# A pool of short columns (128 bytes a partition) is opened in front of the pool of split weights

## The chip, the core and the metric

The kernel runs on one core of a Trainium2 chip. The metric is the device time of one execution, in microseconds (us). Each engine of the core has its own instruction stream: TensorE (PE in the profile, with its weight loads as PEld), VectorE (DVE), ScalarE (ACT), GpSimd (POOL) and SyncE (SP, which issues most of the DMAs).

## The reference

One sequence of 256 tokens of width 1024 goes through five stages, all in float32:

```python
x = x + hgrn_gmlp_mixer(x)     # mixer 0: x@w_in (1024 x 3072), gated recurrence, gMLP, @w_out
x = x + peer_ffn(x)            # 16384 experts, 8 heads, top 16 of each
x = x + mla_moba_mixer(x)      # mixer 1: two kinds of attention, @w_out
x = x + peer_ffn(x)
# second block: z = rmsnorm(x) @ w_in (1024 x 8192); pooling branch, dilated attention, gates
x = x + (gate_a * (y_a @ w_proj_a) + gate_b * (y_b @ w_proj_b)) @ w_out
return rmsnorm(x) * final_gain
```

In `peer_ffn` each token takes, for each of 8 heads, the 16 best of 16384 experts; the output is the sum over the chosen experts of gate * gelu(x . down[e]) * up[e].

## The kernel before

**Products of split numbers.** A float32 product is made of three float32r matmuls (`mm3`, lines 423 to 426): every operand is kept as a high part and a low part, and hi\*hi, hi\*lo and lo\*hi are added up in PSUM. The parts of the weights are made on the core by `split_weights` (line 484): ScalarE writes the high part `wh` from the loaded block, VectorE (sometimes GpSimd) writes the low part `wl`. One block is 128 partitions by 1024 floats, 4096 bytes in each partition.

**Where these parts lie.** The pool `ws` (line 376) has five buffers of `wh` and five of `wl`, opened once in `Net.__init__` and used by all five stages. The mixers have a small pool `w` of their own beside it (three more pairs), and `Stream.advance` gives each unit of weights a buffer of the one or the other. Loaded, unsplit blocks lie in `raw` (expert tables) and `wraw` (the other weights). `esm` (line 379) holds the short columns of the norms that join two stages: `ess` (16 bytes), `ev`, `ey` and `ea` (4 bytes each), each in a place of 32 bytes.

**The expert stage** (`peer`, line 1086, run twice) does not gather experts. It goes over all 128 blocks of 128 experts. `project(e)` makes 24 matmuls of 256 columns per block, with `xh` or `xl` (the token vectors) as the moving operand and `wh` or `wl` of the down table as the stationary one: tiles `ps<-xh,wh`, `ps<-xl,wh`, `ps<-xh,wl`. 40 blocks are projected while VectorE picks the top 16 (`front`), 60 while the gates are spread over the experts by one-hot matmuls (`acc<-oo,ah`), and 28 in the last part. That last part, `expand(e, tb, n)`, makes 12 matmuls of 512 columns per block, with `wh` or `wl` of the up table moving and the gated activations `W` (hi and lo of one block) stationary: tiles `acc<-wh,W` and `acc<-wl,W`. For the last four blocks all of these parts lie in one tile of another pool, called `places`, and the same 12 matmuls are shown as `acc<-places`.

**Mixers and the second block** run lists of `Lin` jobs. A job of kind "T" has the tokens moving and the weights stationary (`acc<-xh,wh`), one of kind "N" has the weights moving and the tokens stationary (`acc<-wh,xh`); 24 matmuls make one output piece. `N2` is the output product of a mixer, 512 columns wide (`acc<-wh,mh`).

All matmuls are recorded at line 421. The order is written out by hand (`manual_schedule`); each engine works through its own list in order.

Of the kernel before, what the change touches and what calls it, by code (L numbers as in the profile page):

```python
# [109 lines left out]
class Lin:  # L110
# [5 lines left out]
    def __init__(self, x, W, nk, cols, cn, kind, cb, late=0, k0=0, acc=None, start=True, stop=True,  # L116
                 need=None, mid=None, of=None, pieces=None):
        self.x, self.W, self.nk, self.cn, self.kind, self.cb, self.late = x, W, nk, cn, kind, cb, late
        self.mid, self.of = mid, of
        self.pieces = pieces or range({"T": cn // 128, "N": 2, "N2": 4}[kind])  # L120
        self.k0, self.acc, self.start, self.stop, self.need = k0, acc, start, stop, need
        self.cols = cols if isinstance(cols, tuple) else (cols, cn, 1, cn)
        self.w, self.keep = [], False
        if of:
            of.keep = True
# [240 lines left out]
class Net:  # L366
    def __init__(self, ctx, tc, A):
        self.tc, self.nc, self.A, self.ctx = tc, tc.nc, A, ctx
        nc = self.nc
        P = lambda name, **k: ctx.enter_context(tc.tile_pool(name=name, **k))  # L370
        self.cp = P("consts", bufs=1)
        self.raw = P("raw", bufs=4)
        self.dram = P("dram", bufs=1, space=DRAM)
        self.n = 0
        cp = self.cp
        self.ws = P("ws", bufs=WS)
        self.pa = P("pa", bufs=4, space=PSUM)
        self.pb = P("pb", bufs=4, space=PSUM)
        self.esm = P("esm", bufs=1)
        self.xn = [cp.tile([128, KB, S], F32R, name=n) for n in ("xh", "xl")]  # L380
        self.ident = cp.tile([128, 128], F32, name="ident")
        nc.scalar.dma_start(self.ident, A["c_ident"])
        self.vec = cp.tile([128, NVEC], F32, name="vec")
        self.entry = self.brow = None
# [1502 lines left out]
```

## Time and profile before

| what | value |
|---|---|
| time, median of 3 runs | 2179.43 us (2176.91 to 2179.50) |
| the profiled execution's own time | 2180.57 us |
| its span on the core | 2178.5 us |
| PE busy | 2122.6 us (97%) |
| DVE busy | 1568.8 us (72%) |
| ACT busy | 1125.7 us (52%) |
| mean granted clock of TensorE | 0.994 of full speed |

A matmul's duration in the profile is modelled and reaches beyond the start of the next one, so the rate of TensorE is read here from the starts: the time between two starts, called the pace below. Where a pace is worked out from rows of the timeline, it is the difference of two start times divided by the number of matmuls between them.

### The profile page before, as it was taken

The page shows a single profiled execution, that of the slowest core. Times are in us where ns is not written, and L with a number is a line of the kernel's source. Part 1 is how long each engine was busy: PE and PEld are TensorE (multiplying, and loading weights), DVE is VectorE, ACT ScalarE, POOL GpSimd, SP SyncE. Part 2 cuts the span into 40 slices and gives each one's busy share as a digit, 9 for nine tenths or more (in the row PEclk, how much of TensorE's full clock was granted, in tenths as well). Part 3 has the DMA queues.
Part 4 walks back from the last instruction along what each step waited for, and adds up shares of the span by engine and source line. Part 5 has one row for each costly group of instructions (what it writes and reads, how often), then busy time and mean ns, then how long its engine had stood idle before and what let it go on. Part 6 is the DMA issues. An engine that isn't in the chain of part 4 may idle for free.

```text
span 2178.5 us, 37618 instructions
## 1 busy us (share of the span) xinstructions
PE 2122.6 (97%) x14793; PEld 1932.1 (89%) x14793; DVE 1568.8 (72%) x2898; ACT 1125.7 (52%) x1944; POOL 215.7 (10%) x133
## 2 busy tenths in 40 slices
PE   7899999999999999998999999999999999999998
PEld 6879999999888888987799999998888889899998
DVE  7968978997555565668679789986666656644565
ACT  6245655554444444557455655555555555554443
POOL 2520110000000000013202200000000000122223
PEclk9999999999999999999999999999999999999999
DMA  7555454455666665744264545446666657475443
GB/s 233 185 185 184 145 194 146 156 159 161 188 189 190 188 195 192 260 129 148 87 233 135 195 149 162 155 155 188 189 187 190 194 193 261 148 218 153 136 146 115
DMA packets 165581, 382.19 MB, mean 175 GB/s; under 512 B 13137, under 2 KB 82444, under 8 KB 165148
## 3 DMA queue, kind: packets, MB, share of 16 engines
q1 hardware_dynamic: 160544, 364.95, 53.0%
q0 software_dynamic: 4672, 14.76, 1.9%
q8 instruction: 116, 1.90, 0.4%
q14 instruction: 61, 0.50, 0.1%
q10 hardware_dynamic: 188, 0.09, 0.0%
HBM read 376.56 MB, written 8.43 MB: 177 GB/s over the span
## 4 chain that ended last, share of the span: by engine, by line
PE 86%; DVE 9%; ACT 3%; issue 1%; DMA 0%; DVEq 0%; ACTq 0%
PE acc L421 53%; PE ps L421 29%; DVE wl L488 2%; ACT wh L487 1%; PE bsc L421 1%; PE bo L421 1%; DVE qL L678 1%; PE ps L200 1%; PE sc L421 0%; PE bpt L1747 0%; DVE eq L1278 0%; DVE s L1195 0%; DVE CI L1200 0%; DVE SC L658 0%; ACT scr L873 0%
## 5 line engine op out<-in xcount | busy, mean ns | idle before, releaser
L488 DVE TENSOR_TENSOR wl<-raw,wh 128x1024 fp32r<-128x1024 f32 x484 | 600.0, 1249 | 135.2 <-ACT wh L487 134.4
L421 PE MATMUL acc<-wh,W 128*128 128x512 f32 x1984 | 630.8, 395 | 0.0
L421 PE MATMUL ps<-xh,wh 128*128 128x256 f32 x2048 | 579.1, 283 | 0.0
L421 PE MATMUL ps<-xl,wh 128*128 128x256 f32 x2048 | 572.9, 280 | 0.0
L421 PE MATMUL ps<-xh,wl 128*128 128x256 f32 x2048 | 572.6, 280 | 0.0
L487 ACT ACTIVATE wh<-raw 128x1024 fp32r<-128x1024 f32 x504 | 526.9, 1054 | 74.2 <-PE ps L421 55.4
L421 PEld LDWEIGHTS acc<-wh,W 128*128 128x128 f32 x1984 | 373.4, 188 | 85.6 <-DVE W L1431 0.4
L421 PE MATMUL acc<-wl,W 128*128 128x512 f32 x992 | 391.5, 395 | 0.0
L421 PEld LDWEIGHTS ps<-xh,wh 128*128 128x128 f32 x2048 | 385.2, 188 | 2.4
L421 PEld LDWEIGHTS ps<-xl,wh 128*128 128x128 f32 x2048 | 385.1, 188 | 2.1
L421 PEld LDWEIGHTS ps<-xh,wl 128*128 128x128 f32 x2048 | 385.2, 188 | 0.0
L421 PEld LDWEIGHTS acc<-wl,W 128*128 128x128 f32 x992 | 186.7, 188 | 42.0 <-DVE wl L488 0.3
L1430 ACT ACTIVATE W<-ZB 128x256 fp32r<-128x256 f32 x168 | 91.4, 544 | 184.7 <-PE acc L421 161.0
L487 ACT ACTIVATE wh<-wraw 128x1024 fp32r<-128x1024 f32 (+1 forms) x140 | 144.4, 1043 | 46.5 <-PE acc L421 38.2
L1431 DVE TENSOR_TENSOR W<-ZB,W 128x256 fp32r<-128x256 f32 x168 | 89.8, 534 | 108.4 <-ACT W L1430 108.4
L488 DVE TENSOR_TENSOR wl<-wraw,wh 128x1024 fp32r<-128x1024 f32 (+2 forms) x104 | 132.8, 1284 | 45.9 <-ACT wh L487 45.7
L421 PE MATMUL acc<-xh,wh 128*128 128x256 f32 x480 | 136.2, 284 | 0.0
L421 PE MATMUL acc<-xh,wl 128*128 128x256 f32 x480 | 133.4, 278 | 0.0
L421 PE MATMUL acc<-xl,wh 128*128 128x256 f32 x480 | 133.3, 278 | 0.0
L181 POOL TENSOR_TENSOR ZB<-X,gain 128x512 f32<-128x512 f32 x4 | 5.2, 1293 | 1293.9 <-ACT ZB L179 1293.9
L1474 ACT ACTIVATE ZB<-acc 128x352 f32<-128x352 f32 (+30 forms) x128 | 47.7, 373 | 123.1 <-PE acc L421 119.3
L421 PE MATMUL acc<-wh,xh 128*128 128x256 f32 (+2 forms) x336 | 107.9, 321 | 0.9 <-ACT scr L873 0.9
(409 smaller groups left out, 3114.2 us busy)
## 6 DMA issues: line engine op xcount, KB each, us to landing
raw<-in_l_down_t_dram SPq DMA_DIRECT2D x256, 512.0 KB, 4.3
raw<-in_l_peer_expert_up_dram SPq DMA_DIRECT2D x248, 512.0 KB, 4.3
wraw<-in_l_w_in_dram SPq DMA_DIRECT2D x36, 512.0 KB, 5.1
wraw<-in_w_in_dram SPq DMA_DIRECT2D x36, 512.0 KB, 3.9
wraw<-in_l_peer_w_query_dram SPq DMA_DIRECT2D x32, 512.0 KB, 5.3
wraw<-in_w_in_dram SPq DMA_DIRECT2D x48, 256.0 KB, 3.3
wraw<-in_l_w_out_dram SPq DMA_DIRECT2D x16, 512.0 KB, 4.2
brow<-row POOLq DMA_DIRECT2D x1, 5120.0 KB, 33.6
```

What stands on the lines that cost most here:

```text
L181: nc.gpsimd.tensor_tensor(y, x, self.gB[:, ns], op=OP.mult)
L200: nc.tensor.transpose(q[:, k * 128:k * 128 + 128], self.work[tb][:, (k0 + k) * 128:(k0 + k) * 128 + 128], self.net.ident)
L421: self.nc.tensor.matmul(*a, **k)
L487: self.nc.scalar.activation(hi, r, AF.Copy)
L488: (eng or self.nc.vector).tensor_tensor(lo, r, hi.bitcast(F32), op=OP.subtract)
L678: nc.vector.tensor_tensor(qL, q, Wt, op=OP.mult)
L1430: nc.scalar.activation(h, act, AF.Copy)
L1431: nc.vector.tensor_tensor(l, act, h.bitcast(F32), op=OP.subtract)
L1474: nc.scalar.activation(ZB[:, f - E0:, t4], pv[:, f:], AF.Copy, scale=1.0 / GSC)
```

## The change

One line moves up in `Net.__init__`:

```diff
         cp = self.cp
+        self.esm = P("esm", bufs=1)
         self.ws = P("ws", bufs=WS)
         self.pa = P("pa", bufs=4, space=PSUM)
         self.pb = P("pb", bufs=4, space=PSUM)
-        self.esm = P("esm", bufs=1)
```

Pools are stacked in SBUF in the order in which they are opened. `esm` takes 4 x 32 = 128 bytes of each partition. So the ten buffers of `ws` move up by 128 bytes, and the four columns of `esm` move down by 40,960 bytes into the place in front of them. Pools opened later begin where they began. The programs built from both files have the same instructions in the same order with the same waits on all five engines, and nothing but these addresses is different.

The table gives the start of each tile within its partition, as a remainder after division by 256 bytes, from the built programs. (Slices of these tiles begin at multiples of 512 bytes from the start, so they have the same remainder.)

| tile | before | after |
|---|---|---|
| `wh`, `wl` in `ws` | 64 | 192 |
| `wh`, `wl` in the mixers' own pool `w` | 192 | 192 |
| `xh`, `xl` (tokens) | 128 | 128 |
| `W` (activations of the expert stage) | 192 | 192 |
| `places` (parts of the last four blocks) | 192 | 192 |
| `mh`, `ml`, `ch`, `cl` (operands of the mixers' output products) | 192 | 192 |
| `yh`, `yl`, `bh`, `bl`, `mgh`, `mgl` (second block) | 64 | 64 |
| `w` (query weights in the expert stage) | 64 | 64 |
| `raw` | 64 | 64 |

Below, the distance of a matmul is the remainder of its stationary operand minus that of its moving operand, modulo 256. For three stretches of the timeline it matters which buffers the program uses. Between 29.59 and 34.58 us (kind T) all weights lie in the pool `w`. In the piece from 60.68 to 63.44 us (kind N) the first 12 matmuls have weights in `ws`, the 12 from 62.14 us in `w`. In the output product of mixer 1 the 12 matmuls from 1069.77 us have weights in `ws`, the nine from 1072.57 in `w`, and the three from 1074.63 in `ws` again.

## Rows read from the trace of the kernel before

**Rows 1.** The page: the chain that ended last, by line.

```profile
PE acc L421 53%; PE ps L421 29%; DVE wl L488 2%; ACT wh L487 1%; PE bsc L421 1%; PE bo L421 1%; DVE qL L678 1%; PE ps L200 1%; PE sc L421 0%; PE bpt L1747 0%; DVE eq L1278 0%; DVE s L1195 0%; DVE CI L1200 0%; DVE SC L658 0%; ACT scr L873 0%
```

**Rows 2.** Stretches of the expert stage: length, busy time of each engine, PEclk, DMA share, GB/s.

```profile
150.00:327.00 177.00, 169.06 (x1393) 166.11 (x1392) 147.57 (x483) 93.88 (x136) 31.86 (x16) 0.99 0.56 186
327.00:527.00 200.00, 200.00 (x1938) 198.66 (x1937) 181.09 (x304) 102.45 (x239) 0.00 (x0) 1.00 0.49 154
527.00:835.00 308.00, 308.00 (x1398) 252.74 (x1398) 183.44 (x223) 152.69 (x223) 0.00 (x0) 1.00 0.61 190
835.00:952.00 117.00, 117.00 (x764) 106.29 (x764) 69.89 (x90) 59.85 (x90) 0.00 (x0) 1.00 0.63 210
```

**Rows 3.** Groups of matmuls: count | busy us, mean ns of one | idle before.

```profile
L421 PE MATMUL acc<-wh,W 128*128 128x512 f32 x1984 | 630.8, 395 | 0.0
L421 PE MATMUL ps<-xh,wh 128*128 128x256 f32 x2048 | 579.1, 283 | 0.0
...
L421 PE MATMUL acc<-wl,W 128*128 128x512 f32 x992 | 391.5, 395 | 0.0
```

**Rows 4.** One stretch, matmuls on tile W alone (columns as rows 2).

```profile
560.00:660.00 100.00, 100.00 (x432) 81.09 (x431) 15.32 (x36) 15.03 (x36) 1.00 0.62 188
```

**Rows 5.** Timeline of PE, last four blocks: start us, us, what, count.

```profile
952.78 7.42 PE L421 MATMUL acc<-places 128*128 128x512 f32 x32
```

**Rows 6.** Timeline of PE, output product of mixer 1.

```profile
1069.77 0.39 PE L421 MATMUL acc<-wh,mh 128*128 128x512 f32 x1
...
1072.57 0.39 PE L421 MATMUL acc<-wh,mh 128*128 128x512 f32 x1
...
1073.95 0.39 PE L421 MATMUL acc<-wh,mh 128*128 128x512 f32 x1
...
1074.63 0.40 PE L421 MATMUL acc<-wh,mh 128*128 128x512 f32 x1
```

**Rows 7.** Timeline of PE, a projection among the one-hot matmuls (47 starts).

```profile
343.87 0.37 PE L421 MATMUL ps<-xh,wh 128*128 128x256 f32 x1
344.07 0.28 PE L421 MATMUL ps<-xl,wh 128*128 128x256 f32 x1
...
349.49 0.28 PE L421 MATMUL ps<-xh,wl 128*128 128x256 f32 x1
```

**Rows 8.** Timeline of PE, mixer 0, kind T (45 starts).

```profile
29.59 0.28 PE L421 MATMUL acc<-xh,wl 128*128 128x256 f32 x1
...
34.58 0.28 PE L421 MATMUL acc<-xl,wh 128*128 128x256 f32 x1
```

**Rows 9.** Timeline of PE, mixer 0, kind N (10 starts, then 11).

```profile
61.01 0.28 PE L421 MATMUL acc<-wh,xl 128*128 128x256 f32 x1
...
62.03 0.28 PE L421 MATMUL acc<-wh,xl 128*128 128x256 f32 x1
62.14 0.28 PE L421 MATMUL acc<-wh,xh 128*128 128x256 f32 x1
...
63.32 0.28 PE L421 MATMUL acc<-wl,xh 128*128 128x256 f32 x1
```

**Rows 10.** Timeline of PE, second block, kind T, two pieces (53 starts; 22 starts).

```profile
1943.06 0.28 PE L421 MATMUL acc<-xh,wh 128*128 128x256 f32 x1
...
1948.95 0.28 PE L421 MATMUL acc<-xl,wh 128*128 128x256 f32 x1
...
2012.63 0.28 PE L421 MATMUL acc<-xl,wh 128*128 128x256 f32 x1
...
2015.11 0.28 PE L421 MATMUL acc<-xl,wh 128*128 128x256 f32 x1
```

**Rows 11.** Timeline of PE, second block, output product (25 starts).

```profile
2149.00 0.28 PE L421 MATMUL acc<-wl,mgh 128*128 128x256 f32 x1
...
2151.88 0.28 PE L421 MATMUL acc<-wl,mgh 128*128 128x256 f32 x1
```

**Rows 12.** Low parts on DVE: count, duration ns min/median/max, first and last start.

```profile
L488 DVE TENSOR_TENSOR wl<-raw,wh x484: 1194/1225/3391, 168.0 to 1875.3; 128x1024 fp32r<-128x1024 f32 x162
L488 DVE TENSOR_TENSOR places<-ZB,places x8: 1218/1218/1222, 899.6 to 1848.7; 128x1024 fp32r<-128x1024 f32 x8
```

## The prediction

> **What bounds the kernel now.** I read the page's chain first, then the stretches, then the pace of TensorE's matmuls. The chain is TensorE: its matmuls into `acc` hold 53% of the span and those into `ps` 29% [rows 1]. The stretches say where nothing else counts: from 327 to 952 us PE is busy for the whole of each stretch at a granted clock of 1.00, with VectorE at 181 of 200 us in the first of them and at 60% in the next two [rows 2]. So in most of the kernel the time is a number of matmuls times their pace, and anything that alters the pace by a few ns is seen in full. Two kinds make up most of it: 1,984 + 992 = 2,976 matmuls of 512 columns on `W`, and 3 x 2,048 = 6,144 of 256 columns into `ps` [rows 3].
>
> No instruction, wait or DMA is moved, so the only thing the change can act on is how an address meets another. Hence the question to the trace: does the pace of one and the same shape depend on where its operands lie? It does.
>
> With 512 columns, rows 6 hold the clearest place. In one output product of mixer 1 the weights change buffers while the other operand stays at remainder 192. From 1069.77 to 1072.57 us the weights are in `ws` (64): 12 matmuls in 2.80 us, 233.3 ns each. The nine that follow have them in the pool `w` (192), and the last three of these take 0.68 us, 226.7 ns each [rows 6]. The `places` matmuls, all at 192, go at the same pace: 32 of them begin within 7.42 - 0.39 us, so (7.03 / 31) 226.8 ns [rows 5]. The `W` matmuls, with `wh` at 64 and `W` at 192, have 432 in a stretch of 100 us; with the 0.395 us that one lasts [rows 3] that is 100.4 / 432 = 232.4 ns [rows 4]. Distance 0 thus goes at 226.7, distance 128 at 232 to 233.
>
> With 256 columns the tokens are at 128, and the distance is 64 one way round or the other. There are two paces, and once TensorE has fallen into one it keeps it, mostly until the next break. At distance 192 (`ps` today) it is 117.8 ns: 46 steps in 5.42 us [rows 7]. At distance 64, in mixer 0 with the weights in its own pool, it is 113.4 ns: 44 steps in 4.99 us [rows 8]. Within one piece of kind N the pace goes from 113.3 (distance 64) to 118.0 (distance 192) at the matmul where the buffers change [rows 9]. But it isn't the distance alone: the second block runs distance 192 at 113.3 in one piece and at 118.1 in another [rows 10]. What is set by the distance is which of the two it tends to after a break. In the trace 12 starts after a break at distance 64 can be followed at full clock, and nine of them settled at 113 within six matmuls; of the starts at distance 192 in the expert stage nearly all settled at 118. At distance 0 a 256-column matmul takes 120.0 ns: 24 steps in 2.88 us [rows 11].
>
> **The change part by part.** `ws` goes from 64 to 192. Each kind of matmul gets another distance.
>
> `W` matmuls: 128 becomes 0, the case of rows 5 and of the end of rows 6. 232.4 - 226.8 = 5.6 ns, times 2,976 = 16.7 us less. The bounds are 0 (the quiet engines around `places` make the pace) and 18 us (233.3 to 226.7 and some more). I take 16.7: the operands of rows 5 stand exactly where these will stand, and rows 6 show the same in a busy stage.
>
> Projections into `ps`: 192 becomes 64. All at 113.4 would save 4.4 ns each. Of 128 blocks 40 are in the first part, where VectorE sets part of the time (148 of 177 us busy, PE 169) [rows 2]; these 40 x 24 x 2 = 1,920 I count by half, 4.2 us. The other 4,224 give 18.6 us. Together 22.8 us; the lower bound is 0, since after a one-hot matmul no start at distance 64 is shown and it may lock to 118 as now. From the nine in 12 I take a share of 0.65: 14.8 us less.
>
> Second block, kind T: at present at both paces [rows 10], afterwards two thirds fast: some 1,200 matmuls, a share moved by a quarter at most, about 1 us less (between 3 less and 2 more). `yh`, `bh` and `mg`: 0 becomes 128, 6 x 32 + 3 x 64 = 384 matmuls now at 120.0 [rows 11]. With 256 columns that distance isn't shown; between 113.4 (2.5 us less) and 6.6 ns more as with 512 columns (2.5 us more) I take 1 us more. Kind N in `ws`: 64 becomes 192; about 270 now at 113 go to 118, 1.2 us more. The 512-column matmuls on `xh` change sides as well, about 190, unknown: 1.3 us either way, taken as 0.
>
> Splits: ACT and DVE read and write other remainders. A low part made with everything at 192 took 1218 ns, the median of those with everything at 64 is 1225 [rows 12]; and nobody waits for them from 327 us on. Nothing. `esm` holds columns of at most 16 bytes: nothing.
>
> Sum: -16.7 - 14.8 - 1 + 1 + 1.2 = -30.3 us. The profiled execution took 2180.57 us, so 2150.3; it lies 1.1 us over the median of the runs, which gives 2149 us. The cover for this gain is VectorE from 327 to 527 us: 181 us busy there would be 93% of a stretch that is some 5 us shorter, still under TensorE.
>
> Against all of this stands a rule of the Trainium skill (SBUF — State Buffer, section "Who interferes with whom"): TensorE has one read port for the moving operand and another, independent one for weight loads, and "PE and ACT never wait on anyone". By it an address would be of no account, and the time would stay. The trace doesn't agree: 226.7 against 233.3 ns in one product [rows 6] is what it doesn't allow for.
>
> **The rivals.**
>
> Only `W` gains. The projections come out of the one-hot matmuls with a phase that locks to 118 at distance 64 also. For it: three of the 12 starts did so. Against it: rows 8. Then -16.7 with the small terms at +2 leaves 2180.6 - 14.7 - 1.1 = 2165 us.
>
> Nothing happens. The paces come from what surrounds a matmul (breaks, what the other engines do), and buffers only happened to change at the same moments. For it: two paces at one distance [rows 10]. Against it: the change of pace at the very matmul in rows 6 and 9. 2179 us.
>
> Slower. What counts is the remainder of the `ws` operand by itself, 192 the slow one for 256 columns, and 226.8 at `places` is owed to idle DVE and ACT. For it: rows 9, where 192 is the slow half. Then `W` gains nothing, and what now goes at 113 beside `ws` (about 1,000 matmuls of the second block, the mixers and a few blocks of the expert stage) loses 4.5 ns each, 4.5 us; `yh`, `bh`, `mg` and the 512-column ones add up to 4: 2188 us. It decides only if rows 8, with 192 on the fast side, were chance.
>
> **How the numbers follow.** The forecast (`W` at 227 and at least half of the projections at 113) has a chance of 0.60; only `W`, 0.22; nothing, 0.09; slower, 0.06; the remaining 0.03 is a gain eaten by another limit, near 2172. Everything fast would be -16.7 - 22.8 - 3 - 2.5 + 0, 2135 us; I set the low end at 2137, and the high end at 2168, so that it takes in the case of `W` alone. This kernel's runs can tell about 0.2%, 4.4 us, from no change. Faster by more: 0.60 + 0.22 + 0.03 = 0.85. Within it: 0.09. Slower: 0.06.
>
> **What would show it.** `acc<-places` at 226.8 as now and `acc<-wh,W` at the same pace, its mean duration about 389 to 390 ns in place of 395; a stretch of 100 us with 442 of them and not 432. The mean of `ps` between 276 and 279 ns in place of 280 to 283, with blocks of 24 wholly at 113 or wholly at 118. DVE's and ACT's own durations unchanged. The prediction is wrong if `W` stays at 232, and its larger half is wrong if `ps` stays at 118 throughout.

## The result and the profile after

The kernel after takes 2153.89 us (median of 4 runs, 2151.36 to 2154.89) against 2179.47 us (2176.91 to 2179.76) of the kernel before in the same comparison: a ratio of 0.9883, 95% interval 0.9866 to 0.9901, 25.6 us less.

| what | before | after |
|---|---|---|
| the profiled execution's own time | 2180.57 us | 2151.36 us |
| its span on the core | 2178.5 us | 2149.2 us |
| PE busy | 2122.6 us (97%) | 2092.5 us (97%) |
| DVE busy | 1568.8 us (72%) | 1565.1 us (73%) |
| ACT busy | 1125.7 us (52%) | 1124.3 us (52%) |
| mean granted clock of TensorE | 0.994 | 0.997 |

The chain that ended last, by line, on the page after (it answers to [rows 1]):

```profile
PE acc L421 52%; PE ps L421 29%; DVE wl L488 3%; ACT wh L487 1%; DVE qL L678 1%; PE bsc L421 1%; PE bo L421 1%; DVE eq L1278 1%; PE ps L200 1%; PE sc L421 0%; DVE eq L1281 0%; DVE eq L1274 0%; DVE s L1195 0%; PE bpt L1747 0%; DVE CI L1200 0%
```

The same two groups of matmuls hold the end, and the share of `acc` is a point lower. The groups of matmuls (count | busy us, mean ns of one | idle before; [rows 3]):

```profile
L421 PE MATMUL acc<-wh,W 128*128 128x512 f32 x1984 | 619.5, 389 | 0.0
L421 PE MATMUL ps<-xh,wh 128*128 128x256 f32 x2048 | 579.3, 283 | 0.0
...
L421 PE MATMUL acc<-wl,W 128*128 128x512 f32 x992 | 386.0, 389 | 0.0
```

The `W` matmuls went from 395 to 389 ns each. The mean of the `ps` matmuls did not move: these durations are modelled, and they hide what the starts show below. Next a stretch of 100 us inside the `W` stage, matmuls on that tile alone (length, then PE, PEld, DVE and ACT busy us with counts; [rows 4]), and after it the `places` matmuls (start us, us, what, count; [rows 5]):

```profile
560.00:660.00 100.00, 100.00 (x443) 82.81 (x442) 15.46 (x37) 15.47 (x37) 1.00 0.64 194
```

```profile
939.82 6.74 PE L421 MATMUL acc<-places 128*128 128x512 f32 x29
```

443 matmuls stand where 432 stood: 100.39 / 443 = 226.6 ns. The `places` matmuls, whose addresses did not change, are as they were: (6.74 - 0.39) / 28 = 226.8 ns. The timeline of PE in the output product of mixer 1 ([rows 6]), the first and the last of 37 starts:

```profile
1049.80 0.39 PE L421 MATMUL acc<-wh,ml 128*128 128x512 f32 x1
...
1057.96 0.39 PE L421 MATMUL acc<-wh,ml 128*128 128x512 f32 x1
```

36 steps in 8.16 us are 226.7 ns throughout. The step from 233.3 to 226.7 that the kernel before showed where its weights changed buffers is gone, since both buffers now lie at 192.

The projections are another matter. Here is one among the one-hot matmuls, 48 starts ([rows 7]), and then one behind two transposes of `sel`, 74 starts up to the last row:

```profile
343.70 0.36 PE L421 MATMUL ps<-xh,wh 128*128 128x256 f32 x1
343.90 0.28 PE L421 MATMUL ps<-xl,wh 128*128 128x256 f32 x1
...
349.32 0.28 PE L421 MATMUL ps<-xh,wl 128*128 128x256 f32 x1
```

```profile
261.39 0.41 PE L1289 MATMUL ps<-ident,sel 128*128 128x128 f32 x2 [1.25 <-DVE sel L1283]
261.55 0.37 PE L421 MATMUL ps<-xh,wh 128*128 128x256 f32 x1
261.76 0.28 PE L421 MATMUL ps<-xl,wh 128*128 128x256 f32 x1
...
269.92 0.28 PE L421 MATMUL ps<-xl,wh 128*128 128x256 f32 x1
```

In the first the 46 steps from 343.90 take 5.42 us, 117.8 ns, exactly as before. In the second the 72 steps from 261.76 take 8.16 us, 113.3 ns. Both have distance 64. The kernel does hold both paces, but not in the shares that were forecast.

**Where the time came from.** The steps from one start to the next, all those under 260 ns, are summed by kind over each trace. Some steps of 256 columns fell where the granted clock was 0.5 (1.2 GHz in place of 2.4), and took 207 ns in the mean there: 38 of kind N and 17 of `ps` before (11.4 us together), 27 of kind N after (5.6 us). Their number differs also between kernels with the same distances (all_up32, below, has none of kind N and 34 of `ps`), so one column gives the difference at full clock: that of the mean steps outside these stretches, times the number of matmuls.

| kind | before | after | difference | at full clock | forecast |
|---|---|---|---|---|---|
| `W`, mean 232.57 and 226.72 ns | 691.4 us | 673.8 us | -17.6 us | -17.4 us | -16.7 us |
| `ps`, at 115 ns or less: 284 and 1,473 of some 6,136 | 729.9 us | 723.1 us | -6.8 us | -5.1 us (118.68 to 117.85 ns) | -14.8 us |
| kind T | 170.1 us | 168.5 us | -1.6 us | -1.4 us | -1 us |
| kind N, 256 columns | 93.2 us | 92.3 us | -0.9 us | 0.0 us (118.12 ns in both) | +1.2 us |
| `yh`, `bh`, `mg` | 45.9 us | 45.6 us | -0.3 us | -0.4 us | +1 us |
| query products (`w`, not moved) | 68.5 us | 67.2 us | -1.3 us | -1.3 us | 0 |
| 512 columns on `xh` and on `mh` (about 170 each, by their means) | | | -1.2 us | -1.2 us | 0 |
| sum | | | -29.7 us | -26.8 us | -30.3 us |

Two such stretches of the kernel before, the first in kind N, the second in `ps` (PEclk is the third column from the end); ahead of them TensorE had waited 2.22 and 2.37 us for VectorE:

```profile
95.00:99.00 4.00, 4.00 (x24) 4.00 (x23) 4.00 (x5) 0.00 (x0) 1.84 (x1) 0.58 0.41 131
252.00:256.00 4.00, 3.85 (x20) 3.88 (x21) 3.31 (x3) 3.27 (x6) 1.81 (x1) 0.58 0.62 181
```

The two profiled executions differ by 29.2 us, the medians of the runs by 25.6: the one of before was longer than any of the four runs it is compared by, the one of after was the shortest of its four. The 26.8 us at full clock are nearer to the medians.

### The profile page after: what moved, and what is told of

Read it like the earlier page. It is cut to its first block, busy times and chain, and to the rows that moved or that the text cites. A ratio compares the mean times of both kernels' runs of the same rounds, so it can differ in the third digit from the quotient of the medians.

```text
span 2149.2 us, 37618 instructions
## 1 busy us (share of the span) xinstructions
PE 2092.5 (97%) x14793; PEld 1918.9 (89%) x14793; DVE 1565.1 (73%) x2898; ACT 1124.3 (52%) x1944; POOL 217.6 (10%) x133
## 4 chain that ended last, share of the span: by engine, by line
PE 85%; DVE 11%; ACT 3%; issue 1%; DMA 0%; DVEq 0%; ACTq 0%
PE acc L421 52%; PE ps L421 29%; DVE wl L488 3%; ACT wh L487 1%; DVE qL L678 1%; PE bsc L421 1%; PE bo L421 1%; DVE eq L1278 1%; PE ps L200 1%; PE sc L421 0%; DVE eq L1281 0%; DVE eq L1274 0%; DVE s L1195 0%; PE bpt L1747 0%; DVE CI L1200 0%
## 5 line engine op out<-in xcount | busy, mean ns | idle before, releaser
L421 PE MATMUL acc<-wh,W 128*128 128x512 f32 x1984 | 619.5, 389 | 0.0
L421 PE MATMUL acc<-wl,W 128*128 128x512 f32 x992 | 386.0, 389 | 0.0
L1474 ACT ACTIVATE ZB<-acc 128x352 f32<-128x352 f32 (+30 forms) x128 | 47.6, 372 | 123.3 <-PE acc L421 119.4
L488 POOL TENSOR_TENSOR wl<-wraw,wh 128x1024 fp32r<-128x1024 f32 (+1 forms) x36 | 87.0, 2419 | 222.9 <-ACT wh L487 215.6
```

Source lines behind the costliest of these rows:

```text
L421: self.nc.tensor.matmul(*a, **k)
L488: (eng or self.nc.vector).tensor_tensor(lo, r, hi.bitcast(F32), op=OP.subtract)
L1474: nc.scalar.activation(ZB[:, f - E0:, t4], pv[:, f:], AF.Copy, scale=1.0 / GSC)
```

## The experiments

All kernels but three differ from before or after in addresses alone: their instructions, order and waits are the same. Distances are given as `ps` / `W`. An engine's pace in a block behind the one-hot matmuls is read as in [rows 7]: 46 steps, from the second start of two blocks to the 48th.

**1. Distance, or the place of the weights alone.** Theory A: the distance between a matmul's two operands sets its pace. Theory B (the prediction's rival "slower"): the remainder of the `ws` operand by itself does. Three kernels tell them apart. In the first, `esm` is opened ahead of everything, so the tokens move up with `ws`: `ws` at 192 as in the kernel after, but the distances 192 / 0.

```diff
+        self.esm = P("esm", bufs=1)     # now ahead of the pool of constants
...
-        self.esm = P("esm", bufs=1)
```

> The kernel before with the pool of short columns opened first of all: xh/xl at remainder 0, ws at 192, W at 192. So the W matmuls get distance 0, as in the changed kernel, while kind T and ps keep distance 192, as before. Theory A (the distance of a matmul's two operands sets its pace): W at 226.7 ns, ps at 117.9 with some 5% of its matmuls at 113, time about 2162 us (before, less 17). Theory B (the remainder of the ws operand by itself): W at 226.7 and ps as in the changed kernel with a quarter at 113, about 2154 us.

Measured: 2160.8 us, ratio 0.992 (0.9904 to 0.9937). Its timeline of PE among the one-hot matmuls:

```profile
348.32 0.28 PE L421 MATMUL ps<-xl,wh 128*128 128x256 f32 x1
...
353.74 0.28 PE L421 MATMUL ps<-xh,wl 128*128 128x256 f32 x1
```

46 steps in 5.42 us: 117.8 ns, and only 54 of 6,138 steps of `ps` in the whole kernel are at 115 ns or less. `W` is at 227.3 ns. So with the weights at 192 `W` gains and `ps` doesn't, which B can't give. Kind N, whose tokens moved too, went to distance 64: 116.05 ns in the mean at full clock (118.12 before).

In the second kernel the column tile `vec` goes in front of the tokens, so that these move from 128 to 64 and `ws` stays: distances 0 / 128.

```diff
         self.esm = P("esm", bufs=1)
+        self.vec = cp.tile([128, NVEC], F32, name="vec")
...
-        self.vec = cp.tile([128, NVEC], F32, name="vec")
```

> The kernel before with the 192 bytes of vec put in front of xh and xl: only xh, xl and ident move (xh to 64); ws stays at 64, W at 192. W keeps distance 128; ps and kind T get distance 0. Theory A: W at 232.4 as before; ps at 120.0, as yh and mg went at distance 0; about 13 us slower than before, 2192 us. Theory B: nothing changes for W or ps, 2179 us.

Measured: 2193.39 us, ratio 1.0068 (1.0052 to 1.0085). The stretch on `W`, as above, and a projection among the one-hot matmuls:

```profile
560.00:660.00 100.00, 100.00 (x432) 81.04 (x432) 15.31 (x36) 15.03 (x36) 1.00 0.61 188
```

```profile
350.97 0.28 PE L421 MATMUL ps<-xl,wh 128*128 128x256 f32 x1
...
356.48 0.28 PE L421 MATMUL ps<-xh,wl 128*128 128x256 f32 x1
```

432 as before the change, and 46 steps in 5.51 us, 119.8 ns; 5,530 of 6,138 steps are at 120 ns to the ns. No weight moved, and `ps` has the pace that the products on `mg` had at distance 0 [rows 11].

The third kernel moves everything up by 32 bytes and leaves all distances alone.

```diff
+        P("pad", bufs=1).tile([128, 8], F32, name="pad")   # ahead of the pool of constants
```

> The kernel before with 32 unused bytes in front of everything: every tile moves by 32 bytes, every distance stays. Theory A: all paces as before, 2179 us within 4. Theory B: with ws at 96 and no operand at its old remainder the paces of W and ps change, by some us at least either way.

Measured: 2178.63 us, ratio 1.0002 (0.9992 to 1.0011); `W` at 233.0 and `ps` at 119.3 ns in the mean (232.6 and 118.9 before; at full clock `ps` is at 118.8 and 118.7). A shift that all tiles share does nothing. Theory B falls.

**2. Other distances.** The same edits combined, and a pad of 32 bytes ahead of or behind `ws` (`vec` ahead of the tokens; the pad ahead of `ws`; the pad behind `ws`; in t32_w0 and t224_w0 `esm` is opened ahead of everything besides). They ask whether a distance exists that beats 64 / 0, and whether 0 alone is good for `W`.

```diff
         self.esm = P("esm", bufs=1)
+        P("pad", bufs=1).tile([128, 8], F32, name="pad")   # t96_w0, t224_w0, t32_w0, t160_w0
         self.ws = P("ws", bufs=WS)
+        P("pad", bufs=1).tile([128, 8], F32, name="pad")   # t64_w32
...
+        self.vec = cp.tile([128, NVEC], F32, name="vec")   # t128_w0, t32_w0, t160_w0: ahead of the tokens
```

> The changed kernel with vec put in front of xh and xl: xh at 64, ws and W at 192. W keeps distance 0; ps and kind T get 128. Theory A: W at 226.7; ps changes, a distance of 128 having cost about 16 cycles over distance 0 with 512 columns: between 118 and 126 ns, so 2154 to 2200 us. Theory B: as the changed kernel, 2154 us.

> W at distance 0 as in the changed kernel, ps and kind T at distance 32 (esm, vec and then xh, xl first; 32 unused bytes in front of ws). Theory A with places of 64 bytes (half a step in distance): ps between its paces at distance 0 (120) and 64 (113 or 118). If only whole steps of 64 bytes count, ps as at distance 0, 120.5, time about 2174 us. W 226.7 either way.

> The changed kernel with 32 unused bytes in front of ws: W at distance 0, ps and kind T at 96, between 64 (117.9 on average, 2154 us) and 128 (120.2, 2174 us). Theory A: W 226.7, and a time between these two, unless distances off a step of 64 are worse for both; theory B (remainder of ws by itself, now 224): W changes.

> esm first of all and 32 unused bytes in front of ws: W at distance 0, ps and kind T at 224, between 192 (118, 2161 us) and 0 (120.9, 2175 us). Theory A: W 226.7, time 2155 to 2178 us; what is open is whether a half step lets ps lock to 113.

> The changed kernel with 32 unused bytes behind ws: ps and kind T at 64 as in the changed kernel, W at distance 32. Theory A: ps as in the changed kernel (a quarter at 113), W between 226.7 (distance 0) and the unknown pace at 64: if the pace rises with the distance, about 228 to 230, time 2156 to 2166 us; if distance 0 is special, 232 and 2171 us.

> The kernel after with the column tile in front of the tokens (tokens at remainder 64) and 32 bytes of pad ahead of the split weights (at 224, as are the W activations): distance 160 for the 256-column matmuls, 0 for W, 64 to 192 untouched elsewhere. By the theory that the distance sets the pace, W is at 226.7 to 227.5, and the projections are no faster than in the mixtures that the distances 96 and 128 gave (mean 120.15 and 120.2): 2166 to 2175 us, 0.995 to 0.998. A version that beats the kernel after is there if distance 160 locks to 113: 2138 us, 0.982.

| label | time, us | ratio (95%) | `W`, ns | `ps` behind one-hots, ns | sum of `ps` steps, us | mean step of `ps` at full clock, ns |
|---|---|---|---|---|---|---|
| t32_w0 | 2169.54 | 0.9960 (0.9946 to 0.9975) | 227.5 | 118.3 | 732.5 | 119.4 |
| t96_w0 | 2168.09 | 0.9955 (0.9938 to 0.9972) | 226.8 | 118.7 | 737.5 | 119.7 |
| t128_w0 | 2173.55 | 0.9976 (0.9966 to 0.9986) | 227.4 | 118.7 | 737.7 | 120.0 |
| t160_w0 | 2179.74 | 1.0004 (0.9994 to 1.0014) | 227.4 | 119.9 | 744.4 | 121.0 |
| t224_w0 | 2158.52 | 0.9911 (0.9895 to 0.9928) | 227.1 | 116.7 | 725.9 | 117.9 |
| t64_w32 | 2173.70 | 0.9979 (0.9967 to 0.9990) | 233.2 | 117.8 | 723.4 | 117.2 |

The sums hold the steps at half clock too, 0 to 42 of some 6,137 in these traces; the last column leaves them out (the kernel after has 117.9 there).

Two of the blocks in the table, of t224_w0 and of t64_w32; the second is one of the last part, whose 24 matmuls follow `W` matmuls without a break:

```profile
347.06 0.28 PE L422 MATMUL ps<-xl,wh 128*128 128x256 f32 x1
...
352.43 0.28 PE L422 MATMUL ps<-xh,wl 128*128 128x256 f32 x1
```

```profile
818.07 0.28 PE L422 MATMUL ps<-xh,wh 128*128 128x256 f32 x1
...
820.69 0.28 PE L422 MATMUL ps<-xh,wl 128*128 128x256 f32 x1
```

At distance 224 the 46 steps take 5.37 us, 116.7 ns. Each distance has a pace, or a cycle of paces, of its own: at 128, 96 and 160 steps of 115 to 125 ns alternate, and their mean is worse than either pace of distance 64. For `W` a distance of 32 is no better than 128: the gain is at 0 alone, of the three tried. The block of t64_w32 takes 2.62 us for 23 steps, 113.9 ns with its entry; by the median step of each block all 1,344 matmuls behind `W` are on the fast pace there, where in the kernel after 1,320 of 1,344 are on the slow one:

```profile
795.27 0.28 PE L421 MATMUL ps<-xh,wh 128*128 128x256 f32 x1
...
797.98 0.28 PE L421 MATMUL ps<-xh,wl 128*128 128x256 f32 x1
```

(the kernel after, 23 steps in 2.71 us, 117.8 ns). Distance and code of these blocks are equal in the two kernels, and the `W` matmuls ahead of them run at another pace. That this pace is the cause is not shown: the tiles that the pad moves by 32 bytes, `W` among them, are read and written by other engines as well, and no kernel but this one tries another pace of `W` at distance 64. t160_w0 was to beat the kernel after if 160 had a fast pace; it has not, and its 2179.74 us lie above the 2166 to 2175 us that were expected.

**3. What chooses between the two paces of distance 64.** In the kernel after all 1,152 matmuls behind the transposes of `gt` and `sel` are on the fast pace, 2,832 of 2,880 behind one-hot matmuls on the slow one, as are the 528 behind `ps<-skT,qTp`. Theory C: the transposes do it. So one is put in between.

```diff
                         pgs.append(pg.rearrange("p j i -> p i j"))
+                    self.brk = True
...
                 pP = self.ps()[:, :S]
+                if getattr(self, "brk", False):
+                    self.nc.tensor.transpose(pP[:, :128], self.ident, self.ident)
+                    self.brk = False
```

> The kernel after, with one transpose of the 128x128 identity on TensorE (into the PSUM tile that the projection then overwrites) between the one-hot matmuls and the first projection behind them, 64 in all; addresses unchanged. Theory: a block of 256-column matmuls at distance 64 has two stable paces, and what TensorE did just ahead of the break chooses; behind transposes all 1,152 matmuls of the kernel after went at 113, behind one-hot matmuls 2,832 of 2,880 at 118. Then these 2,832 go at 113.4: 4.4 ns each, 12.5 us less, and 64 transposes at some 55 ns (the pace of the one on gt) cost 3.5 us: about 9 us under the kernel after, 2145 us, 0.984 of the kernel before; about 4,200 of 6,144 at 115 ns or less. Rival: the place in the kernel decides (what DVE and ACT read and write in that stage), not what went ahead: the blocks stay at 118, and the transposes only cost, 2157 us, 0.990.

Measured: 2159.64 us, ratio 0.991 (0.9893 to 0.9928). Its timeline of PE:

```profile
347.01 0.28 PE L1128 MATMUL ps<-ident 128*128 128x128 f32 x1
347.04 0.36 PE L421 MATMUL ps<-xh,wh 128*128 128x256 f32 x1
347.24 0.28 PE L421 MATMUL ps<-xl,wh 128*128 128x256 f32 x1
...
352.66 0.28 PE L421 MATMUL ps<-xh,wl 128*128 128x256 f32 x1
```

46 steps in 5.42 us: 117.8 ns. 2,808 of 2,880 stay slow, and the transposes only cost. Theory C falls. One thing differs from the transposes of `sel` above: those came after 1.25 us in which TensorE waited for VectorE, this one comes straight behind a matmul.

Theory D: the operands of the first matmuls choose. The three products of a step are put in another order.

```diff
-                    self.mm3(pP, (dh[:, k], dl[:, k]), (xh[:, k], xl[:, k]), k == 0, k == KB - 1)
+                    self.mm(pP, dl[:, k], xh[:, k], start=k == 0, stop=False)
+                    self.mm(pP, dh[:, k], xh[:, k], start=False, stop=False)
+                    self.mm(pP, dh[:, k], xl[:, k], start=False, stop=k == KB - 1)
```

> The kernel after, with the three products of each step of a projection in another order: low weights on high tokens, high on high, high on low (before: high on high, high on low, low on high), as in no other place; addresses and counts unchanged. If the entry of a block (which operands the first matmuls behind the break have) chooses the pace, blocks behind one-hot matmuls or behind W change sides: all of the 4,150 that go at 118 there to 113.4 would be 18 us less, 2136 us, 0.980; the blocks behind transposes could fall back to 118, 5 us more, 2159 us, 0.991. If only what went ahead of the break counts, nothing moves: 2154 us, 0.988, about 1,470 of 6,144 at 115 ns or less.

Measured: 2156.59 us, ratio 0.9899 (0.9881 to 0.9917). All 2,880 behind one-hots and 1,296 of 1,344 behind `W` are slow. D falls as well for these. Of the 1,152 behind transposes 360 became slow, but that needs no new order: 264 are slow in the next kernel too, which has the old one.

Theory E: VectorE's traffic in that stage holds the slow pace. Its two products that spread the gates are left out.

```diff
-                        nc.vector.scalar_tensor_tensor(ZA[:, :, t4], pv[:, :E0], 1.0 / GSC, ZA[:, :, t4],
-                                                       op0=OP.mult, op1=OP.mult)
-                        if f > E0:
+                        if f < 0:
```

> The kernel after without the two VectorE products that spread the gates (PSUM times ZA or ZB, 1/GSC), so that the gates of most experts are left out of the result; TensorE's list, the addresses and all other work are unchanged. It asks whether VectorE's traffic beside them holds the projections among the one-hot matmuls at 118 ns. If it does, those 2,832 matmuls go at 113.4 and the two front parts of the stage lose 12.5 us: about 2141 us, 0.983 of the kernel before. If TensorE's own sequence holds them there, they stay at 117.9 and the time stays near that of the kernel after, since VectorE bounds little from 327 to 527 us: 2150 to 2154 us, 0.987 to 0.988.

Measured: 2157.2 us, ratio 0.9896 (0.9877 to 0.9915). The stretch from 327 us, of no_spread and then of the kernel after ([rows 2]):

```profile
327.00:527.00 200.00, 200.00 (x1932) 198.37 (x1931) 155.28 (x180) 101.19 (x240) 0.00 (x0) 1.00 0.49 153
```

```profile
327.00:527.00 200.00, 200.00 (x1900) 197.25 (x1899) 179.31 (x302) 103.24 (x239) 0.00 (x0) 1.00 0.51 155
```

DVE is down from 179 to 155 us, and 2,832 of the 2,880 matmuls are still slow. The time lies above the 2150 to 2154 us expected for this case; 44 steps of `ps` fell at half clock (9.2 us), none in the trace of the kernel after. E falls for these products; VectorE's remaining 155 us and ScalarE's 101 us were not taken away.

The same kernel shows something else. Up to 320 us it is the kernel after, instruction for instruction and address for address. Yet its first block behind `sel` is slow:

```profile
266.75 0.38 PE L1289 MATMUL ps<-ident,sel 128*128 128x128 f32 x2
266.89 0.36 PE L421 MATMUL ps<-xh,wh 128*128 128x256 f32 x1
267.09 0.28 PE L421 MATMUL ps<-xl,wh 128*128 128x256 f32 x1
...
274.28 0.28 PE L421 MATMUL ps<-xh,wl 128*128 128x256 f32 x1
```

61 steps in 7.19 us are 117.9 ns, against 113.3 in the kernel after. There TensorE had waited 1.25 us ahead of the transposes, and the first step of the block took 0.21 us; here it had not waited, and the first step took 0.20 us. TensorE came to it later: in a stretch ahead its granted clock was 0.67 in the mean, with PE busy for 3.11 of 6 us, so between the two levels of 1.2 and 2.4 GHz (the kernel after has 1.00 in that place, from 246 to 252 us):

```profile
250.00:256.00 6.00, 3.11 (x15) 3.14 (x16) 4.97 (x9) 5.97 (x10) 1.09 (x1) 0.67 0.68 182
```

The five kernels at distance 64 (after, t64_w32, tr_oo, lo_first, no_spread) have 362 blocks behind a break that ran wholly at full clock. In 16 the first step was 205 ns or more, and all 16 are fast; of the 346 with a shorter one 17 are. What goes with the fast pace is thus how the block is entered, at the scale of some 4 ns. That is an association: no run set that step on purpose, and why it is 206 ns and not 202 is open.

No kernel tried beats the kernel after. lo_first (2156.59 us) and, without the gates, no_spread (2157.2 us) come nearest, and their intervals overlap with its own; of those that differ in addresses alone it is t224_w0 with 2158.52 us.

## Why the prediction was right

**The cause.** Right, and shown: the time hangs on the distance between the two operands, and neither on the place of the weights (t192_w0, t0_w128) nor on addresses as such (all_up32). The rivals "nothing" and "slower" fall with that. What in TensorE or in SBUF makes the distance count stays open. The rule of the Trainium skill weighed in the prediction (SBUF — State Buffer, section "Who interferes with whom"), read as it was there, that an address is of no account to TensorE, is contradicted more strongly than by the trace of before: kernels with one instruction list run from 2153.89 to 2193.39 us, by addresses alone.

**`W`.** Right: 5.85 ns for 2,976 matmuls, 17.4 us, where 5.6 ns and 16.7 us were forecast. The operands of [rows 5] and of the end of [rows 6] were the right neighbours.

**The projections.** The share was wrong. "From the nine in 12 I take a share of 0.65": the share of fast steps in the trace is 24% (5% before), and at full clock the sum went down by 5.1 us, not 14.8: 0.22 of the 22.8 us. The nine starts of 12 were starts outside the expert stage, since no projection and no query product had distance 64 before; the larger part of the 6,144 stands behind one-hot matmuls (2,880) and behind `W` (1,344), where distance 64 fell into 117.8 nearly always. The lower bound, "after a one-hot matmul no start at distance 64 is shown and it may lock to 118 as now", was the case there. The blocks of the first part, counted by half, were the ones that gained: 1,392 of their 1,920 matmuls are on the fast pace now. The expected mark, a mean of `ps` between 276 and 279 ns, did not come (280 to 283, as before); that blocks are wholly at 113 or wholly at 118 did.

**The small terms.** Forecast +1.2 us in all, measured -4.3 us at full clock. `yh`, `bh` and `mg` at distance 128 take 119.4 ns in the mean instead of 120.3 (bounds 113.4 and 126.6, the value taken above the middle). Kind N was to lose 1.2 us and lost nothing. One piece of mixer 0 did what was forecast and is now slow from its second start to its last ([rows 9] had the first half at 113.3):

```profile
59.23 0.28 PE L421 MATMUL acc<-wl,xh 128*128 128x256 f32 x1
...
61.82 0.28 PE L421 MATMUL acc<-wh,xl 128*128 128x256 f32 x1
```

22 steps in 2.59 us, 117.7 ns; over the kernel other pieces made up for it (118.12 ns in both traces). The 512-column matmuls gained 1.2 us. Those on `xh` had been taken as 0; those on `mh` were missing from the sum, though [rows 6] show them at 233.3 with weights in `ws`. The query products gained 1.3 us: 294 of 576 steps are at 115 ns or less, none before, though neither of their operands had moved and their distance is still 192. So what goes on around a matmul counts beside its distance, as the rival "nothing" had it for the whole; what it is there isn't shown.

**The sum.** The agreement is in part luck: 9.7 us of gain in the projections did not come, and 0.7 us more in `W` and 5.5 us more in the small terms made up for over half of it. That leaves 26.8 us at full clock for the forecast 30.3. By the medians it is 25.6 us, and 2153.89 us against the forecast 2149. The nearer agreement of the two profiled executions, 29.2 us, is owed to which executions were profiled.

**The splits.** Right: VectorE's low part took 1225 ns in the median [rows 12] and takes 1224 now (the row of the line's own view, count and ns min/median/max):

```profile
L488 DVE TENSOR_TENSOR wl<-raw,wh x484: 1196/1224/3229, 165.9 to 1847.4; 128x1024 fp32r<-128x1024 f32 x162
```

**The rival "only `W`".** It was given 2165 us and is what t192_w0 built, but for kind N: 2160.8 us. The kernel after, at 2153.89 us, lies between this rival and the forecast: `W` gained in full, and the projections about a third of their term.

## What to carry to other kernels

Where TensorE is the bound, read the pace of each shape from the starts, leave out stretches with a lower granted clock, and hold it against the operands' addresses modulo 256 bytes (no run here tests whether the pattern repeats after just 256): here 512-column matmuls gained 2.5% when both operands began at the same remainder, while 256-column ones were worse there than at 64 apart. Place the tiles for the kind that has most matmuls and check the others. Where one shape shows two paces at one distance, don't carry the share of one stage to another: count it behind each kind of predecessor.

## What had not been expected

- A step of 32 bytes in the distance, the smallest tried, already acts, and differently for the two widths. 512 columns: 226.7 ns at 0, 233.2 at 32, 232.6 at 128. 256 columns, behind one-hots: 119.8 at 0, 118.3 at 32, 117.8 or 113.3 at 64, 118.7 at 96 and at 128, 119.9 at 160, 117.8 at 192, 116.7 at 224.
- The pace of a block may hang on the pace of what ran ahead without a break: at distance 64, behind `W` at 226.7 ns 1,320 of 1,344 matmuls went at the slow pace, behind `W` at 233.2 ns all 1,344 at the fast one. It is one kernel against another, and not shown to be the cause.
- Two programs that are equal up to 320 us, addresses too, ran the same block ahead of that at 113.3 ns in one execution and at 117.9 in the other, after a wait of 1.25 us and after none. What sets this, and whether it can be forced behind the one-hot matmuls, stays open; by the paces above I estimate its worth there at 2,832 x 4.4 ns = 12.5 us.
